# Stick-breaking attention in a two-block kernel: query tiles in rising order, scores one tile at a time, more projection chunks between them

## Chip, cores and metric

The kernel runs on one core of a Trainium2 chip. The metric is the device time of one execution in microseconds (us), as the median of several runs. The engines are TensorE (PE; PEld is its weight load), VectorE (DVE), ScalarE (ACT), GpSimd (POOL) and SyncE (SP), which issues the DMAs. Each engine works through its own queue in order.

## What is computed

Two transformer blocks on a sequence of T = 1024 with D = 1024, in fp32. The first block projects the normed input to the columns of three branches, two of them gated linear attention and the third stick-breaking attention with four heads of width 64, and projects the joined outputs. The second block (sparse and latent attention, feed-forward) is not touched by the change. The part that the change is about:

```python
def stick_breaking_attn(q, k, v):
    scale = dh ** -0.5
    for i in range(t // SB_BLOCK):                     # SB_BLOCK = 128
        n_keys = (i + 1) * SB_BLOCK
        z = jnp.einsum('bhtd,bhsd->bhts', q_blk, k[:, :, :n_keys]) * scale
        strict = s_pos < t_pos
        log_beta = jax.nn.log_sigmoid(z)
        log_1m_beta = jnp.where(strict, jax.nn.log_sigmoid(-z), 0.0)
        between = lax.cumsum(log_1m_beta, axis=3, reverse=True) - log_1m_beta
        weights = jnp.where(strict, jnp.exp(log_beta + between), 0.0)
        outs.append(jnp.einsum('bhts,bhsv->bhtv', weights, v[:, :, :n_keys]))
...
def first_block(...):
    h = rms_norm(x) * (1.0 + scale) + shift
    p = h @ w_in
    (qa, ka, va, lra, ga, qb, fb, ib, gb, qc, kc, vc, gc) = split_columns(p)
    o_a = rms_norm(chunk_gated_linear_attn(qa, ka, va, log_alpha)) * gla_norm_w * silu(ga)
    o_b = rms_norm(chunk_gated_linear_attn(silu(qb), k_b, ib, log_f)) * hgrn_norm_w * silu(gb)
    o_c = stick_breaking_attn(qc, kc, vc) * silu(gc)
    x = x + gate * (jnp.concatenate([o_a, o_b, o_c]) @ w_out)
```

## The kernel before, in words

**Chunks.** Matmuls run in a split form: each operand is a rounded part and a remainder, and three products are added. After the first columns, the rest of the first block's input projection is cut into 50 chunks in a queue, `fq`. A chunk of `unit_f` has 24 matmuls 128x512 (L515 to L517, PSUM tile `F_ps`), one of `unit_v` 48 matmuls 128x256 (L242 to L244, `v_ps`). `fill()` issues the next chunk at the place where it is called, and loads the weights (raw tile from DMA, ACT's cast L209, POOL's subtraction L210). Two PSUM buffers serve all chunks. ACT copies a finished chunk to a staging tile (L500, `F_st`, `v_st`) and SP stores it; the four chunks of the values `vc` are instead split into two parts by ACT (L958) and DVE (L959). Four chunks are issued ahead of the heads loop, 18 in it, and 28 in the steps of the linear attention behind it, one in each of 28 steps.

**Stick-breaking attention** (L817 to L941). The 32 query tiles of four heads are handled as 16 items (head, pair `ip` of tiles); tile t = 2 ip + w has 128 (t + 1) keys. `prep` (L826) loads and splits a head's queries and keys (ACT L835 and L837, DVE L836, POOL L838). For one tile `stage_a` makes the scores in PSUM (`sb_pb`, two buffers; L850, L851, mask L852) and ACT's Abs, Exp and Ln (L854 to L856); `stage_b` is DVE's L863, the scan L864 and the subtraction L865, after which the PSUM is free, and ACT's Exp L866. For each of 40 pairs (item, two key blocks) `stage_c` transposes the weights (L217 into `sb_pg`, one buffer), copies them (L882, on ACT or DVE) and splits them on POOL (L883, L884); `stage_d` makes the products L898 into `sb_po`, one buffer for two items; `finish` adds the halves (ACT L911, DVE L914).

**Order around it.** The pairs are taken in the order 0, 3, 2, 1. The scores of four tiles are made before the loop, and in it the two tiles of item i + 2 around the slots of item i; the loop has 40 slots, and `slot * 18 // 40` says behind which of them a chunk is issued. A scheduler places the instructions of each engine from the order of the calls, by modelled readiness.

**The linear attention** behind it runs through 28 levels (4 head pairs of 7), each with four stages that are one step apart: DVE L619, L621 and ACT L622 (a), products with the decay on POOL and DVE (L641, b), PE's L654 (c) and DVE's masked copy L663 into the score tile (d). Each step issues a chunk while there are any. When `fq` is empty, the finished outputs are split for the out-projection (`mix_split`, L760 and L762). The reductions L336 on DVE make the gate's vector while the first chunks run.

## Time and profile before

| | us |
|---|---|
| median of 3 runs (2431.04 to 2431.95) | 2431.05 |
| the profiled execution, its own time | 2437.99 |
| its span in the profile | 2436.2 |
| PE busy in it | 2259.0 (93%) |
| DVE busy | 1433.1 (59%) |
| ACT busy | 895.3 (37%) |
| POOL busy | 1166.3 (48%) |

The profile is one execution of the kernel on the chip; busy times are the union of an engine's instructions, and matmuls are pipelined, so a matmul's own duration is longer than the distance to the next. A row of the waits says what an engine waited for, on which instruction, for how long in all, how often and the longest. In the timelines, a row is start, duration, engine, line, operation and tiles, with the idle time ahead of it in brackets and what ended it. The granted clock is PE's, as a share of full speed: 1.0 is 2.4 GHz, 0.5 is 1.2 GHz.

### The profile page before, as it was taken

The page shows a single profiled execution, that of the slowest core. Times are in us where ns is not written, and L with a number is a line of the kernel's source. Part 1 is how long each engine was busy: PE and PEld are TensorE (multiplying, and loading weights), DVE is VectorE, ACT ScalarE, POOL GpSimd, SP SyncE. Part 2 cuts the span into 40 slices and gives each one's busy share as a digit, 9 for nine tenths or more (in the row PEclk, how much of TensorE's full clock was granted, in tenths as well). Part 3 has the DMA queues.
Part 4 walks back from the last instruction along what each step waited for, and adds up shares of the span by engine and source line. Part 5 has one row for each costly group of instructions (what it writes and reads, how often), then busy time and mean ns, then how long its engine had stood idle before and what let it go on. Part 6 is the DMA issues. An engine that isn't in the chain of part 4 may idle for free.

```text
span 2436.2 us, 30605 instructions
## 1 busy us (share of the span) xinstructions
PE 2259.0 (93%) x11689; PEld 1882.3 (77%) x11689; DVE 1433.1 (59%) x1990; ACT 895.3 (37%) x1467; POOL 1166.3 (48%) x924
## 2 busy tenths in 40 slices
PE   4969989999989999978999998999999999999998
PEld 3748878787768888767778887788888888888886
DVE  8566684848656447899967776535333333333335
ACT  4446632432313244765367777103211111111111
POOL 4236684545446354444357888530334443443341
PEclk9979999979889999989999999999999999999999
DMA  6432231213442112434351442340111111111112
GB/s 256 119 111 74 100 117 70 105 57 133 160 166 87 63 67 96 158 123 116 113 138 44 110 114 92 120 148 31 65 44 52 44 44 52 52 52 44 52 44 80
DMA packets 127200, 226.20 MB, mean 93 GB/s; under 512 B 48818, under 2 KB 73026, under 8 KB 126658
## 3 DMA queue, kind: packets, MB, share of 16 engines
q1 hardware_dynamic: 127042, 224.14, 27.4%
q8 instruction: 94, 1.54, 0.3%
q14 instruction: 64, 0.52, 0.1%
HBM read 169.47 MB, written 54.63 MB: 92 GB/s over the span
## 4 chain that ended last, share of the span: by engine, by line
PE 47%; DVE 8%; ACT 3%; issue 2%; POOL 1%; DMA 1%; SPq 0%; DVEq 0%; ACTq 0%; POOLq 0%
PE up_pb L1980 5%; PE up_pb L1979 5%; PE up_pb L1981 5%; PE br_ps L1925 3%; PE dn_ps L2034 3%; PE dn_ps L2036 3%; PE dn_ps L2035 3%; DVE topk_r L1589 2%; ACT topk_r L1590 1%; PE dn_pb L1980 1%; PE dn_pb L1981 1%; PE dn_pb L1979 1%; PE op_ps L1126 1%; PE op_ps L1125 1%; PE op_ps L1124 1%
## 5 line engine op out<-in xcount | busy, mean ns | idle before, releaser
L2038 DVE TENSOR_TENSOR br_h<-br_h,dn_ps 128x512 f32<-128x512 f32 x176 | 119.7, 686 | 237.4 <-PE dn_ps L2036 237.2
L205 POOL TENSOR_SCALAR up_wh<-up_raw 128x1024 fp32r<-128x1024 f32 x41 | 43.5, 1062 | 273.0 <-PE up_pb L1980 134.0
L2017 DVE SCALAR_TENSOR_TENSOR ffn_ws<-up_pb,cols,ffn_ws 128x1023 f32<-128x1023 f32 x66 | 84.6, 1282 | 138.9 <-ACT ffn_ws L2015 138.0
L2015 ACT ACTIVATE ffn_ws<-up_pb,cols 128x1024 f32<-128x1024 f32 x33 | 40.0, 1211 | 234.9 <-PE up_pb L1981 234.9
L1590 ACT ACTIVATE topk_r<-topk_r 128x896 bf16<-128x896 bf16 (+2 forms) x96 | 90.4, 945 | 61.6 <-DVE topk_r L1589 61.6
L210 POOL TENSOR_TENSOR up_wl<-up_raw,up_wh 128x1024 fp32r<-128x1024 f32 x41 | 98.4, 2401 | 20.2 <-PE up_pb L1981 17.5
L1980 PE MATMUL up_pb<-op_fl,up_wh 128*128 128x512 f32 x264 | 102.8, 389 | 0.0
L1981 PE MATMUL up_pb<-br_h,up_wl 128*128 128x512 f32 x264 | 102.8, 389 | 0.0
L1980 PE MATMUL up_pb<-br_h,up_wh 128*128 128x512 f32 x264 | 102.8, 389 | 0.0
L1981 PE MATMUL up_pb<-op_fh,up_wl 128*128 128x512 f32 x264 | 102.8, 389 | 0.0
L1979 PE MATMUL up_pb<-br_h,up_wh 128*128 128x512 f32 x264 | 102.8, 389 | 0.0
L1979 PE MATMUL up_pb<-op_fh,up_wh 128*128 128x512 f32 x264 | 102.8, 389 | 0.0
L2022 ACT CAST up_g<-ffn_ws 128x1024 fp32r<-128x1024 f32 x22 | 23.1, 1051 | 176.4 <-PE dn_ps L2035 98.0
L2034 PE MATMUL dn_ps<-dn_wh,up_g 128*128 128x512 f32 x192 | 75.2, 392 | 1.2 <-DVE br_h L2038 1.2
L2036 PE MATMUL dn_ps<-dn_wh,up_g 128*128 128x512 f32 x192 | 74.8, 390 | 0.0
L2035 PE MATMUL dn_ps<-dn_wl,up_g 128*128 128x512 f32 x192 | 74.8, 390 | 0.0
L2020 POOL TENSOR_TENSOR ffn_ws<-ffn_ws 128x1024 f32<-128x1024 f32 x22 | 52.7, 2396 | 32.7 <-DVE ffn_ws L2017 32.7
L883 POOL TENSOR_SCALAR sb_tmp<-sb_st 128x512 fp32r<-128x512 f32 (+1 forms) x40 | 36.9, 923 | 60.2 <-ACT sb_st L882 32.0
L1709 POOL TENSOR_TENSOR attB_pt<-attB_r,attB_pt 128x512 fp32r<-128x512 f32 (+1 forms) x54 | 63.5, 1175 | 4.1
L1436 DVE SCALAR_TENSOR_TENSOR c_isc<-idx_r,x_iws,c_isc 128x384 f32<-128x384 f32 (+5 forms) x42 | 46.7, 1111 | 30.5 <-ACT idx_r L1433 28.8
L1709 POOL TENSOR_TENSOR attA_pt<-attA_r,attA_pt 128x512 fp32r<-128x512 f32 (+1 forms) x52 | 61.5, 1183 | 4.0
L1670 DVE TENSOR_SCALAR_CACHE_REDUCE attB_g<-attB_pb 128x1024 f32<-128x1024 f32 (+3 forms) x64 | 47.7, 753 | 26.6 <-PE attB_pb L1663 23.7
(770 smaller groups left out, 7755.9 us busy)
## 6 DMA issues: line engine op xcount, KB each, us to landing
up_raw<-in_wu SPq DMA_DIRECT2D x43, 512.0 KB, 3.2
dn_raw<-in_wu SPq DMA_DIRECT2D x21, 512.0 KB, 3.3
sb_sp<-F_st SPq DMA_DIRECT2D x34, 256.0 KB, 2.0
init_X<-in_wada SPq DMA_DIRECT2D x13, 512.0 KB, 4.6
c_raw<-in_wu SPq DMA_DIRECT2D x13, 512.0 KB, 3.4
sb_raw<-in_wu SPq DMA_DIRECT2D x12, 512.0 KB, 4.3
br_raw<-in_wu SPq DMA_DIRECT2D x12, 512.0 KB, 4.3
bq_raw<-in_wu SPq DMA_DIRECT2D x11, 512.0 KB, 3.5
```

Of the source, the lines that this page charges most:

```text
L210: (nc.gpsimd if pool else nc.vector).tensor_tensor(l, raw, h, op=OP.subtract)
L1590: nc.scalar.activation(y, y, AF.Copy, accum_out=cnt[:, j:j + 1])
L1709: nc.gpsimd.tensor_tensor(lo, x, hi, op=OP.subtract)
L1925: nc.tensor.matmul(po, w[:, ws], x[:, k, hs], start=(n == 0), stop=(n == 11))
L1979: nc.tensor.matmul(o, wh[:, s], self.hh[h][:, kk], start=(kk == 0), stop=False)
L1980: nc.tensor.matmul(o, wh[:, s], self.hl[h][:, kk], start=False, stop=False)
L1981: nc.tensor.matmul(o, wl[:, s], self.hh[h][:, kk], start=False, stop=(kk == KT - 1))
L2017: nc.vector.scalar_tensor_tensor(u[:, d:], p[:, :T - d], tap(2 - d), u[:, d:], op0=OP.mult, op1=OP.add)
L2034: nc.tensor.matmul(po, hi[:, ts], wh[:, cs], start=(k == 0), stop=False)
L2035: nc.tensor.matmul(po, hi[:, ts], wl[:, cs], start=False, stop=False)
L2036: nc.tensor.matmul(po, lo[:, ts], wh[:, cs], start=False, stop=(k == 1))
L2038: nc.vector.tensor_tensor(x, x, po, op=OP.add)
```

## The change

The pairs are taken in rising order 0, 1, 2, 3. The scores of five single tiles are made ahead of the loop, with a chunk behind each of the second to the fifth; then the loop asks ahead of each slot for as many tiles as `5 + slot * 4 // 5` allows, so that four tiles fall on five slots, one at a time. The next head's `prep` is issued ahead of the scores of the second pair's first tile. In the 40 slots there are again 18 chunks, at `slot * 9 // 20`. In all, 26 chunks are issued by the end of the loop in place of 22, and 24 are left for the linear attention, whose last four of 28 steps have none. Because the pairs rise, `finish` writes 512 neighbouring columns. The split of a `vc` chunk is done in two pieces for each engine, of 128x4x64, in place of four of 128x2x64. Lines behind L822 have numbers lower by one.

```diff
-        order = (0, 3, 2, 1)
-        items = [(hd, ip) for hd in range(4) for ip in order]
+        items = [(hd, ip) for hd in range(4) for ip in range(4)]
...
-            po, n, place, end = live["po"], 0, int(ip > 1), 2 * ip + 1
+            po, n, place, end = live["po"], 0, ip % 2, 2 * ip + 1
...
-            if (h, ip) == (0, order[1]):
+            if (h, ip) == (0, 1):
                 live["o"] = self.gt("mx")
...
-            q2 = lambda y: y[hs].rearrange("p (q t) -> p q t", q=2)
-            o = live["o"][hs].rearrange("p (q t) -> p q t", q=4)[:, slice(1, 3) if ip in (1, 2) else slice(0, 4, 3)]
-            nc.vector.tensor_tensor(o, q2(po), q2(t1), op=OP.add)
-            if (h, ip) == (1, order[-1]):
+            nc.vector.tensor_tensor(live["o"][hs, ip // 2 * 512:ip // 2 * 512 + 512], po[hs], t1[hs], op=OP.add)
+            if (h, ip) == (1, 3):
                 done(pair, live["o"])
 
         yield prep(0)
 
-        for i in range(2):
-            for w in (1, 0):
+        ahead = [(i, w) for i in range(len(items)) for w in range(2)]
+
+        def scores(n):
+            while ahead and 2 * len(items) - len(ahead) < n:
+                i, w = ahead.pop(0)
+                if (items[i][1], w) == (1, 0) and items[i][0] < 3:
+                    prep(items[i][0] + 1)
                 stage_a(i, w)
                 stage_b(i, w)
-        behind, slot, slots = [], 0, 4 * 10
+        for n in range(1, 6):
+            scores(n)
+            if n > 1:
+                self.fill()
+        behind, slot = [], 0
         for i, (hd, ip) in enumerate(items):
-            if ip == order[0] and hd < 3:
-                prep(hd + 1)
             for c in range(ip + 1):
-                for w in (((1, 0) if ip == 0 else (1,)) if c == 0 else (0,) if c == (ip + 1) // 2 else ()):
-                    if i + 2 < len(items):
-                        stage_a(i + 2, w)
-                        stage_b(i + 2, w)
+                slot += 1
+                scores(5 + slot * 4 // 5)
                 stage_c(i, c)
                 behind.append((i, c))
-                slot += 1
-                if slot * 18 // slots > (slot - 1) * 18 // slots:
+                if slot * 9 // 20 > (slot - 1) * 9 // 20:
                     self.fill()
...
-                for c in range(2):
-                    nc.scalar.copy(hi[:, c], x[:, c])
-                    nc.vector.tensor_tensor(lo[:, c], x[:, c], hi[:, c], op=OP.subtract)
+                nc.scalar.copy(hi, x)
+                nc.vector.tensor_tensor(lo, x, hi, op=OP.subtract)
```

**Where instructions move.** Each list is the order of one engine's instructions, not a time. The first place is ACT at the start of the heads. Names: `v_ps` and `F_ps` are the chunks' PSUM tiles, `F_st` their staging tiles, `sb_pb` the scores of a tile (128 columns for each key block), `sb_X` and `sb_S` its weights, `sb_wh` a weight block of a chunk, `loga` the decay of the linear attention. Before:

```order
L958 CAST sb_w872_490<-v_ps139_831 128x2x64
L209 CAST sb_wh206_1208<-sb_raw205_1206 128x1024
L492 ACTIVATE loga_tmp135_816<-loga_tmp135_816 128x1024
L958 CAST sb_w872_490<-v_ps139_831 128x2x64
L958 CAST sb_w873_491<-v_ps139_831 128x2x64 x2
L854 ACTIVATE sb_X153_923<-sb_pb152_919 128x256
L855 ACTIVATE sb_X153_923<-sb_X153_923 128x256
L856 ACTIVATE sb_X153_923<-sb_X153_923 128x256
L209 CAST sb_wh209_1214<-sb_raw208_1212 128x1024
```

and some twenty rows later, still before, the first copy of an `F_ps` chunk, `F_ps182`:

```order
L854 ACTIVATE sb_S167_1003<-sb_pb166_997 128x640
L855 ACTIVATE sb_S167_1003<-sb_S167_1003 128x640
L856 ACTIVATE sb_S167_1003<-sb_S167_1003 128x640
L882 COPY sb_st178_1048<-sb_pg176_1042 128x512
L500 COPY F_st183_1083<-F_ps182_1058 128x512
L866 ACTIVATE sb_S165_989<-sb_S165_989 128x768
L866 ACTIVATE sb_S167_1003<-sb_S167_1003 128x640
```

After, the start of the heads:

```order
L958 CAST sb_w872_490<-v_ps139_819 128x4x64
L209 CAST sb_wh172_1027<-sb_raw171_1025 128x1024
L492 ACTIVATE loga_tmp135_804<-loga_tmp135_804 128x1024
L958 CAST sb_w873_491<-v_ps139_819 128x4x64
L500 COPY F_st160_958<-F_ps159_933 128x512
L209 CAST sb_wh175_1033<-sb_raw174_1031 128x1024
L500 COPY F_st168_1010<-F_ps167_985 128x512
L853 ACTIVATE sb_X153_907<-sb_pb152_903 128x128
L854 ACTIVATE sb_X153_907<-sb_X153_907 128x128
L855 ACTIVATE sb_X153_907<-sb_X153_907 128x128
L853 ACTIVATE sb_X155_919<-sb_pb154_915 128x256
L854 ACTIVATE sb_X155_919<-sb_X155_919 128x256
```

The copies of the first two chunks (`F_ps159`, `F_ps167`) now stand ahead of the first Abs of a score tile, and the split of the last `vc` chunk is two rows in place of four; before, the first such copy stood behind the functions of six tiles.

The second place is PE at the first tiles of the second head. Before, with the tiles of 256 and 128 keys (`sb_pb195`, `sb_pb200`), a transpose into `sb_pg` between them and the chunk `F_ps224` behind:

```order
L850 MATMUL sb_pb195_1158<-sb_qkb160_971,sb_qkb161_972 128x256
L851 MATMUL sb_pb195_1158<-sb_qkb160_971,sb_qkb162_973 128x256
L852 LDWEIGHTS idb_118
L852 MATMUL sb_pb195_1158<-neg_475,idb_118 128x128
L217 MATMUL sb_pg202_1196<-idr_116,sb_S167_1003 128x128
L217 MATMUL sb_pg202_1196<-idr_116,sb_S165_989 128x128
L850 MATMUL sb_pb200_1184<-sb_qkb160_971,sb_qkb161_972 128x128
L851 MATMUL sb_pb200_1184<-sb_qkb160_971,sb_qkb162_973 128x128
L852 LDWEIGHTS idb_118
L852 MATMUL sb_pb200_1184<-neg_475,idb_118 128x128
L516 MATMUL F_ps224_1292<-init_hl4_93,sb_wh180_1054 128x512
L517 MATMUL F_ps224_1292<-init_hh2_91,sb_wl181_1055 128x512
```

After, with the tiles of 256 and 384 keys (`sb_pb220`, `sb_pb231`) and matmuls of the chunk `v_ps241`:

```order
L849 MATMUL sb_pb220_1350<-sb_qkb161_961,sb_qkb162_962 128x256
L850 MATMUL sb_pb220_1350<-sb_qkb161_961,sb_qkb163_963 128x256
L851 LDWEIGHTS idb_118
L851 MATMUL sb_pb220_1350<-neg_475,idb_118 128x128
L217 MATMUL sb_pg222_1362<-idr_116,sb_X192_1146 128x128
L244 MATMUL v_ps241_1488<-sb_wh175_1033,init_hl4_93 128x256
L849 MATMUL sb_pb231_1440<-sb_qkb161_961,sb_qkb162_962 128x384
L850 MATMUL sb_pb231_1440<-sb_qkb161_961,sb_qkb163_963 128x384
L851 LDWEIGHTS idb_118
L851 MATMUL sb_pb231_1440<-neg_475,idb_118 128x128
L897 MATMUL sb_po219_1345<-sb_tmp217_1340,sb_w872_490 128x256
L242 MATMUL v_ps241_1488<-sb_wh175_1033,init_hh2_91 128x256
```

Before, no matmul of a chunk stood between the two tiles; after, one does here, while 22 to 38 stand between the tiles of the first head from the fifth on. Later in the phase both kinds occur.

The third place is ACT at the end of the linear attention, where L622 and L624 belong to a level of the linear attention, L701, L262 and L708 to a norm, L760 to the split for the out-projection and L738 to a gate. Before:

```order
L500 ACTIVATE F_st719_4659<-F_ps718_4634 128x512
L622 ACTIVATE gla64_X725_4685<-gla64_X725_4685 128x1024
L738 ACT_TABLE_LOAD
L738 ACTIVATE F_tmp720_4662<-mix_X721_4663 128x1024
L624 ACTIVATE gla64_X729_4730<-gla64_X729_4730 128x512
L760 CAST F_mh732_4761<-mix_tmp736_4765 128x512
L500 ACTIVATE F_st727_4714<-F_ps726_4689 128x512
L760 CAST F_mh732_4761<-mix_tmp737_4771 128x512
L760 CAST F_mh733_4762<-mix_tmp736_4765 128x512
L760 CAST F_mh733_4762<-mix_tmp737_4771 128x512
L500 ACTIVATE F_st731_4758<-F_ps730_4733 128x512
L760 CAST F_mh732_4761<-mix_tmp739_4790 128x512
```

After, the rows around the last copy of a chunk in the first block's projection:

```order
L622 ACTIVATE gla64_X722_4692<-gla64_X722_4692 128x1024
L760 CAST F_mh707_4613<-mix_tmp710_4616 128x512
L760 CAST F_mh707_4613<-mix_tmp711_4622 128x512
L500 ACTIVATE F_st705_4609<-F_ps704_4584 128x512
L701 ACTIVATE go64_tmp717_4648<-go64_mx701_4565 128x1024
L261 ACT_TABLE_LOAD
L760 CAST F_mh706_4612<-mix_tmp719_4667 128x512
L760 CAST F_mh707_4613<-mix_tmp719_4667 128x512
L262 ACTIVATE go64_c715_4646<-go64_pg714_4645,epsc_122 128x16
L708 ACTIVATE go64_c715_4646<-go64_c715_4646 128x16
L760 CAST F_mh706_4612<-mix_tmp720_4673 128x512
L760 CAST F_mh707_4613<-mix_tmp720_4673 128x512
L622 ACTIVATE gla64_X730_4751<-gla64_X730_4751 128x1024
```

Before, copies of chunks (L500) alternate with the splits L760 up to the last level's functions; after, the last one (`F_st705`) stands ahead of a further level's function L622 and most of the splits.

## Rows read from the trace of the kernel before

**Rows 1.** Windows: stretch, its length, busy us (count) of five engines, PEclk, DMA share, GB/s

```profile
117.00:142.00 25.00, 15.40 (x61) 11.85 (x59) 20.80 (x28) 7.01 (x15) 8.00 (x3) 0.84 0.64 225
142.00:170.00 28.00, 14.81 (x50) 10.94 (x50) 20.92 (x18) 17.20 (x22) 11.62 (x9) 0.53 0.14 44
170.00:230.00 60.00, 54.33 (x384) 49.40 (x383) 36.21 (x39) 38.00 (x65) 36.40 (x30) 0.94 0.20 62
230.00:290.00 60.00, 55.66 (x346) 48.81 (x345) 39.03 (x41) 38.71 (x65) 39.84 (x30) 0.94 0.35 123
290.00:351.00 61.00, 50.85 (x320) 44.10 (x318) 48.43 (x40) 29.22 (x42) 52.75 (x36) 0.99 0.25 91
351.00:613.00 262.00, 249.25 (x1437) 208.66 (x1438) 170.90 (x159) 85.01 (x100) 125.56 (x65) 0.91 0.26 92
613.00:651.00 38.00, 37.99 (x248) 32.94 (x247) 30.81 (x30) 16.09 (x21) 13.69 (x10) 1.00 0.38 139
651.00:684.00 33.00, 25.31 (x109) 15.56 (x110) 8.67 (x12) 10.38 (x16) 12.16 (x9) 0.53 0.65 236
684.00:2436.00 1752.00, 1678.77 (x8304) 1399.80 (x8302) 979.21 (x1517) 601.68 (x1043) 823.88 (x712) 0.99 0.25 82
```

**Rows 2.** PE's waits, 117 to 170 us: us in total, times, longest

```profile
PE sb_pb L850 <- DVE sb_X L865: 8.5, 3, 5.8
PE F_ps L515 <- DVE sb_w L959: 6.1, 1, 6.1
PE ada_po L217 <- DVE ada_c L336: 3.5, 1, 3.5
```

**Rows 3.** PE's timeline around the first chunks of the heads

```profile
117.51 0.48 PE L515 MATMUL F_ps<-init_hh,sb_wh 128*128 128x512 f32 x1
...
122.86 0.39 PE L517 MATMUL F_ps<-init_hh,sb_wl 128*128 128x512 f32 x1
129.38 0.77 PE L515 MATMUL F_ps<-init_hh,sb_wh 128*128 128x512 f32 x1 [6.13 <-DVE sb_w L959]
```

**Rows 4.** DVE's timeline, 117 to 142 us

```profile
117.36 3.04 DVE L336 CUSTOM_DVE_ANT_0 ada_X<-ada_X,init_mx 128x1024 f32<-128x1024 f32 x1
...
128.94 0.29 DVE L959 TENSOR_TENSOR sb_w<-v_ps,sb_w 128x128 fp32r<-128x128 f32 x1 [0.33 <-ACT sb_w L958]
...
134.67 0.69 DVE L864 TENSOR_TENSOR_SCAN sb_X<-sb_X 128x256 f32<-128x256 f32 x1
```

**Rows 5.** DVE's timeline at 231 us

```profile
230.68 2.23 DVE L864 TENSOR_TENSOR_SCAN sb_S<-sb_S 128x256 f32<-128x256 f32 x1
```

**Rows 6.** ACT's timeline, 117 to 170 us

```profile
131.73 0.38 ACT L854 ACTIVATE sb_X<-sb_pb 128x256 f32<-128x256 f32 x1 [2.82 <-DMA loga_sp<-loga_X]
...
164.40 0.59 ACT L500 COPY F_st<-F_ps 128x512 f32<-128x512 f32 x1
```

**Rows 7.** PE's waits, 170 to 351 us

```profile
PE sb_pb L850 <- DVE sb_S L865: 5.5, 2, 4.5
...
PE sb_pg L217 <- ACT sb_st L882: 2.5, 1, 2.5
```

**Rows 8.** DVE's groups by line, 613 to 651 us: busy, mean ns, idle before

```profile
L663 DVE COPY_PREDICATED ST<-lv,gla_pb 128x1024 f32<-128x1024 uint8 x6 | 8.9, 1481 | 3.0 <-PE gla_pb L654 3.0
L619 DVE TENSOR_TENSOR gla_X<-go_qkb 128x512 f32<-128x512 f32 x4 | 5.1, 1282 | 0.0
...
L621 DVE TENSOR_TENSOR gla_X<-go_qkb 128x512 f32<-128x512 f32 x3 | 2.1, 689 | 0.0
```

**Rows 9.** ACT's timeline, 608 to 655 us

```profile
623.43 0.60 ACT L500 ACTIVATE F_st<-F_ps 128x512 f32<-128x512 f32 x1
...
648.27 0.59 ACT L500 ACTIVATE F_st<-F_ps 128x512 f32<-128x512 f32 x1
```

**Rows 10.** POOL's groups by line and shape, 117 to 351 us

```profile
L884 POOL TENSOR_TENSOR sb_tmp<-sb_st,sb_tmp 128x512 fp32r<-128x512 f32 x24 | 34.1, 1419 | 1.7
...
L883 POOL TENSOR_SCALAR sb_tmp<-sb_st 128x512 fp32r<-128x512 f32 x24 | 21.2, 885 | 35.0 <-DVE sb_st L882 28.2 <-ACT sb_st L882 6.8
```

## The prediction

> **What bounds the kernel now.** I first read the busy time by stretch [rows 1]. From 684 us to the end TensorE (PE) works 1678.77 of 1752 us at a granted clock of 0.99, and from there on the instructions of every engine stand as they did; only what lies ahead can move. The heads of the attention fill 117 to 351 us. There PE's busy time is 15.40 + 14.81 + 54.33 + 55.66 + 50.85 = 191.05 us of 234, so 43 us are idle, and the first 53 us are the worst: 30.21 us of work, at clocks of 0.84 and 0.53, between 22.8 us of idle time. From 351 to 613 us PE is full (249.25 of 262). In 613 to 651 us PE is full too (37.99 of 38), while VectorE (DVE) is busy for 30.81. The last stretch, 651 to 684 us, is a chain of single steps at half clock.
>
> Next I ask what PE waited for in the first 53 us [rows 2]: 8.5 us until DVE's subtraction L865 gave a score tile's PSUM back, 6.1 us until L959 gave a chunk's PSUM back, 3.5 us for the gate's vector. The 6.1 us are seen one by one [rows 3, 4]: PE ends its chunk at about 123.2, the next starts at 129.38, and the last L959 stands at 128.94, behind a reduction L336 that takes 3.04 us. So the PSUM pair of the chunks is held by a piece that DVE does late, and on ScalarE (ACT) the first Abs of a score tile starts at 131.73 [rows 6]. The chunk that ended at 123.2 is copied out by ACT only at 164.40 [rows 6], behind the functions of six score tiles: all that time one of the two PSUM buffers is simply parked.
>
> **The price of a chunk.** Its first matmul starts at 117.51 and its 24th at 122.86 and takes 0.39 us [rows 3]: 5.7 us with the end, and 5.35 x 24/23 = 5.6 us from start to start. I use 5.6 us for both kinds of chunk.
>
> **The change part by part.** *Four more chunks among the first score tiles.* They take 4 x 5.6 = 22.4 us of PE into this phase and out of the steps of the linear attention. In ACT's new order the copies out of the first two chunks stand ahead of the first Abs, and the merged copies L958 don't alternate with DVE any more, so a buffer comes free before PE asks for the third. By 170 us PE had done some 2.46 chunks, 13.8 us, and about 8 us of scores, transposes and products: 21.8 us of work at full speed in 53. I walked the new orders with the durations of the rows: four chunks back to back from 117.5 to 140 (the first Abs of before starts at 131.73 only, and DVE is busy for 20.80 of the 25 us up to 142, mostly with reductions like L336's, so the scores lose little), then score tiles with a third of a chunk or more between them. That gives about 4.3 more chunks by 170, 24 us, with the attention as far as before; 21.8 + 24 = 46 of 53 us. PE then has no long gap, and the half clock of 142 to 170 (0.53) goes with it. Bounds: if only the 6.1 us of L959, the 3.5 us and half of the 8.5 us fill, 14 us; if all the idle time fills and the clock is full, 53 - 21.8 = 31 us. I take 24, since the order leaves no row behind which a parked buffer stands. The second weight block for these chunks has to be loaded and split earlier; the DMA engines are busy for 0.64 of 117 to 142 [rows 1], so there is room, and were it late the chunks would fall into two and two with a gap like the 6.1 us of before, which is inside these bounds. Of these 24 us the four chunks use 22.4; the sum is **-1.6 us** (+8 to -9).
>
> *The merged pieces L958 and L959.* Four pieces of each become two for the last projection tile; this belongs to the 6.1 us above and is counted there.
>
> *One score tile at a time, in rising order.* From 170 to 351 us the idle time is 5.67 + 4.34 + 10.15 = 20.2 us [rows 1]. The two waits that a pair of tiles makes are named: PE's third tile waits until DVE has worked off the first, 5.5 us, and a transpose waits 2.5 us for ACT's copy, which stands behind a pair's functions [rows 7]. Spacing removes the reason for both: **-8 us**. Bounds: nothing, since in the new order some tiles still stand in pairs with a single projection matmul between them; and -15 with the other waits on the copies and on POOL. No matmul, copy or scan is dropped, so there is no gain in work. The contiguous last addition per pair of items has the same 512 columns as before: 0.
>
> *The preparation of the next head* moves from the head's start to the second tile of its second item. Its four loads, ACT's two casts, the subtraction L836 and POOL's L838 are the same ones, in the same queues, and are wanted only six tiles later: 0, covered by the three or so chunks that lie between. Were the cover gone, the first tile of each of three heads would wait; the nearest row is L850's longest wait, 5.8 us [rows 2].
>
> *The tail of the linear attention.* The queue of chunks is now empty after the 24th of 28 steps. Before, ACT still copied chunks out from 623.43 to 648.27 [rows 9], the first and the last of the four of this stretch, so 4 x 5.6 = 22.4 of PE's 38 us there were chunks. Without them PE has 16 us of work, and the next bound is DVE with 30.81 us [rows 1], most of it L663 at 1.48, L619 at 1.28 and L621 at 0.69 us [rows 8]. So of 22.4 us taken out only 38 - 31 = 7 can come back, and as the six copies of L663 wait for products of PE in turn I take **-6 us**. Bounds: 0, if the chain of steps is as long without chunks; -12, if L619 fell to the 0.69 us of L621 and DVE's other rows lost their company with POOL likewise (some 26 us).
>
> Sum: -1.6 - 8 - 6 = -15.6, rounded to **-15 us**. The profiled execution took 2437.99 us, so it would be 2423; the median of the runs is 7 us lower, 2431.05, and gives **2416 us**.
>
> **What the Trainium skill says against it.** The same scan takes 0.69 us for 256 columns at 134.67 and 2.23 us at 230.68 [rows 4, 5], 1.5 us more, the second beside a subtraction of POOL. The Trainium skill, page "SBUF — State Buffer", section "Who interferes with whom", says that a DVE instruction with two inputs in SBUF contends with a GpSimd instruction that reads SBUF, and that the one issued later waits. By that rule the second scan met POOL, and a denser phase would have more such meetings; the third rival is this mechanism. In 651 to 684 us PE shows a clock of 0.53 although it is busy for 25.31 of 33 us [rows 1], with idle gaps between short steps. The Trainium skill, page "TensorE: Matmul & The Clock Gate", section "What's actually happening", says that the throttled clock is the default and activity releases it. By that rule the chunks keep the tail's clock at 1.00, and taking them away costs what they freed; the second rival is this one.
>
> **The rivals.**
> 1. *All waits go.* The first 53 us fill wholly (-9), the 15 us after 170 go, and the tail falls to -12 with DVE undisturbed; not all at once, so some -30: **2401**. For it: none of these waits is on data that is truly late. Against it: one buffer for transposes and one for products stay.
> 2. *The tail gives nothing back.* PE's 16 us without chunks are 32 at half clock, beside DVE's 31, and each step waits for the other: 38 stay 38. Only the phase of the heads gains, 1.6 + 8: **2422**. For it: 651 to 684 us [rows 1] is just such a stretch. Against it: four stages of the steps are in flight at once.
> 3. *DVE becomes the bound of the heads.* DVE is busy there for 20.80 + 20.92 + 36.21 + 39.03 + 48.43 = 165 us of 234. With tiles spread evenly, scans meet POOL's L884 (1.42 us) and L883 (0.88 us [rows 10]) more often. My forecast leaves the phase at 224 us, so this decides from 59 us more on DVE, 1.5 us for each of the 40 transposed pieces. If each piece cost DVE the 2.2 to 2.3 us that POOL works on it (88 us in all), DVE had 253 us: +19 in place of -9.6, with the tail's -6 some +13: **2444**.
> 4. *The spacing isn't there.* The engines' orders come from a scheduler, and if its pairs stay, only the chunks move: -1.6, and with the tail's 6 lost as in the second rival it is **2430**, no change.
>
> **How the numbers follow.** What tells from no change here is about 0.2%, 4.9 us: faster is below 2426.2, slower above 2435.9. Forecast 0.52, first rival 0.14, second 0.13: faster 0.79. Fourth 0.12: the same. Third 0.09: slower. The range takes the forecast's bounds, the second rival, most of the fourth and the nearer part of the first: 2402 to 2430, which leaves out the third rival and parts of the first and fourth, some 0.2.
>
> **What would show it.** In the changed kernel's profile PE should be busy for over 40 of the 53 us from 117 on, with a clock above 0.9 in 142 to 170, four chunks without a gap over 1 us, and no copy L500 over 10 us late. The wait of L850 (now L849) on DVE after 170 us should fall from 5.5 to under 2 us. The phase of the heads should end at about 341 us (351 less 9.6), with 26 chunks done in place of 22. The last chunk should be copied out some four steps ahead of the end of the linear attention, and the stretch behind it should be one in which DVE is over 0.9 busy. The out-projection, which begins at 684 us before [rows 1], should begin near 669. I am wrong if scans grow so that DVE passes 200 us in the phase (third rival), if PE in the tail is at half clock and DVE idle (second), or if the waits on L865 stay (fourth).

## The result

The changed kernel took 2401.39 us, the median of 4 runs (2395.36 to 2410.10), against 2431.50 (2431.04 to 2436.55) before; the ratio is 0.9874, 95% interval 0.9839 to 0.9910. So it is 30 us faster, twice the 15 us forecast, and 0.6 us below the low end of the range. In a second set of runs it was 2407.15 against 2435.39, ratio 0.9883 (0.9853 to 0.9913). The profiled execution took 2410.10 us, 27.9 less than the profiled execution before, with a span of 2408.2. Both profiled executions are longer than their kernel's median (by 6.5 and 8.7 us), so what follows divides the 27.9 us between two single executions; how the 30 us of the medians divide is known only as far as further profiles repeat it.

The windows of the changed kernel, in the stretches and columns of [rows 1] (stretch, its length, busy us and count of PE, PEld, DVE, ACT and POOL, granted clock of PE, DMA share, GB/s):

```profile
117.00:142.00 25.00, 22.59 (x99) 18.41 (x98) 20.94 (x28) 9.35 (x18) 8.17 (x3) 0.93 0.79 291
142.00:170.00 28.00, 27.53 (x206) 25.23 (x205) 19.22 (x18) 20.66 (x30) 12.12 (x10) 1.00 0.23 68
170.00:230.00 60.00, 55.04 (x341) 47.53 (x340) 42.09 (x47) 37.91 (x67) 44.00 (x32) 0.97 0.28 88
...
351.00:613.00 262.00, 250.49 (x1402) 205.19 (x1400) 176.12 (x177) 97.50 (x117) 129.91 (x70) 0.91 0.26 91
613.00:651.00 38.00, 26.73 (x121) 17.32 (x122) 22.59 (x13) 3.19 (x5) 17.45 (x11) 0.54 0.12 41
```

In the first 53 us PE is now busy for 22.59 + 27.53 = 50.1 us, against 30.2, and the clock of 142 to 170 is 1.00 in place of 0.53. In 613 to 651 it is the other way round: 26.73 us of work at 0.54, where before PE was full at 1.00 [rows 1].

PE's waits of the changed kernel from 117 to 170 us, the answer to [rows 2]: instruction, what it waited for, us in all, times, longest:

```profile
PE F_ps L515 <- DVE sb_w L959: 2.4, 1, 2.4
PE sb_po L897 <- POOL sb_tmp L883: 0.5, 1, 0.5
```

and from 170 to 351 us, the answer to [rows 7]:

```profile
PE sb_pg L217 <- ACT sb_st L881: 5.2, 4, 3.0
PE F_ps L515 <- ACT v_st L500: 3.9, 2, 3.2
...
PE sb_pb L849 <- DVE sb_X L864: 1.5, 4, 0.6
PE sb_pb L849 <- DVE sb_S L864: 1.0, 1, 1.0
```

The waits for a score tile's PSUM (8.5 us ahead of 170, 5.5 behind it) are 0 and 2.5 us. The 3.9 us for a chunk's copy (L500) are new; 3.2 of them lie behind the last product of the heads.

Fixed stretches of the clock cut through different work in the two kernels, so from here on the span is cut at events: the first score matmul; the last product of the heads (345.0 us before, 338.0 after); the linear attention's first masked copy L663 (361.3, 344.4); the last masked copy of its third pair of heads (589.2, 575.2) and of its fourth (651.8, 632.0); the first matmul of the out-projection (683.6, 663.0); the end. "Joint" is what lies between the heads and the first masked copy.

| us, profiled executions | before | after | moved | forecast |
|---|---|---|---|---|
| heads | 228.0 | 220.6 | -7.4 | -9.6 |
| joint | 16.3 | 6.4 | -9.9 | 0 |
| levels of the first three pairs | 227.9 | 230.8 | +2.9 | 0 |
| levels of the fourth pair | 62.6 | 56.8 | -5.8 | -6, with the next |
| their end, to the out-projection | 31.8 | 31.0 | -0.8 | |
| out-projection and all behind it | 1752.6 | 1745.2 | -7.4 | 0 |

The three terms of the sum are there with nearly their sizes, -14.0 in place of -15.6. The other half of the gain lies in two rows for which the forecast had no term. The joint and the three pairs behind it have to be read together, since PE works at chunks in both: counted by their matmuls, the kernel before did 1.46 chunks in the joint and 18.79 in the three pairs, the changed one 0.35 and 19.88. For the same 20.2 chunks the two rows together are 7.0 us shorter.

### The profile page after: what moved, and what is told of

Read it like the earlier page. It is cut to its first block, busy times and chain, and to the rows that moved or that the text cites. A ratio compares the mean times of both kernels' runs of the same rounds, so it can differ in the third digit from the quotient of the medians.

```text
span 2408.2 us, 30577 instructions
## 1 busy us (share of the span) xinstructions
PE 2255.4 (94%) x11689; PEld 1880.8 (78%) x11689; DVE 1413.2 (59%) x1982; ACT 892.4 (37%) x1459; POOL 1169.6 (49%) x924
## 4 chain that ended last, share of the span: by engine, by line
PE 51%; DVE 5%; ACT 2%; issue 2%; POOL 1%; DMA 0%; POOLq 0%; DVEq 0%; ACTq 0%; SPq 0%
PE up_pb L1981 5%; PE up_pb L1979 5%; PE up_pb L1980 5%; PE br_ps L1925 3%; PE dn_ps L2034 3%; PE dn_ps L2036 3%; PE dn_ps L2035 3%; PE F_ps L230 2%; PE F_ps L228 2%; PE F_ps L229 2%; DVE topk_r L1589 2%; PE dn_pb L1980 1%; PE dn_pb L1981 1%; PE dn_pb L1979 1%; PE op_ps L1126 1%
## 5 line engine op out<-in xcount | busy, mean ns | idle before, releaser
L2015 ACT ACTIVATE ffn_ws<-up_pb,cols 128x1024 f32<-128x1024 f32 x33 | 40.0, 1212 | 235.0 <-PE up_pb L1981 235.0
L210 POOL TENSOR_TENSOR up_wl<-up_raw,up_wh 128x1024 fp32r<-128x1024 f32 x41 | 98.5, 2403 | 20.2 <-PE up_pb L1981 17.5
L242 PE MATMUL v_ps<-sb_wh,init_hh 128*128 128x256 f32 x256 | 75.1, 294 | 0.7 <-ACT v_st L500 0.7
L244 PE MATMUL v_ps<-sb_wh,init_hl 128*128 128x256 f32 x256 | 75.3, 294 | 0.0
L243 PE MATMUL v_ps<-sb_wl,init_hh 128*128 128x256 f32 x256 | 74.4, 291 | 0.7 <-POOL sb_wl L210 0.7
L210 POOL TENSOR_TENSOR sb_wl<-sb_raw,sb_wh 128x1024 fp32r<-128x1024 f32 x15 | 39.7, 2651 | 60.3 <-ACT sb_wh L209 41.7
L654 PE MATMUL gla_pb<-QB,gla_X 128*128 128x128 f32 x448 | 62.2, 291 | 6.5 <-POOL gla_X L643 6.5
```

What stands on the lines that cost most here:

```text
L210: (nc.gpsimd if pool else nc.vector).tensor_tensor(l, raw, h, op=OP.subtract)
L242: nc.tensor.matmul(po, hh[:, k, ts], wh[:, cs], start=(k == 0), stop=False)
L244: nc.tensor.matmul(po, hl[:, k, ts], wh[:, cs], start=False, stop=(k == KT - 1))
```

## The parts alone

All kernels of this and the next sections are compared with the kernel before, run beside them; the stretches are of one profiled execution each and stand in a table behind the runs.

**Chunks alone.** To the kernel before, in its old order of tiles:

```diff
             for w in (1, 0):
                 stage_a(i, w)
                 stage_b(i, w)
+                self.fill()
```

> The kernel before with one chunk more behind each of its first four score tiles (26 chunks in the heads, 24 in the linear attention); order and pairs as before. If the chunks are half the gain (my steps): the four chunks cost the phase of the heads 22.4 us and find about that much idle time, so the heads end within 3 us of 351, the tail behind them is 6 to 13 us shorter, 2418 to 2424 us in all. If the chunks are the whole gain, 2401 to 2406 us. If they only displace work (the one parked PSUM buffer is still behind the score functions on ACT), the heads end 10 us or more later and the time is 2428 us or more.

Measured: 2416.53 us against 2435.39, ratio 0.9925 (0.9897 to 0.9952), 18 us faster, just below the first answer's range. The heads were 0.6 us shorter than in the first profile of before with 3.7 chunks more done in them, so the forecast's -1.6 fits; the heads of the old order scatter by 4 us, though (228.0 to 232.3 in the table below). The last levels gave 5.9 us. The rest is the joint (7.2 us) and the stretch behind the out-projection (1748.4).

**Order alone.** The changed kernel without the chunks among its first tiles:

```diff
         for n in range(1, 6):
             scores(n)
-            if n > 1:
-                self.fill()
```

> The changed kernel without the four chunks among its first tiles (22 chunks in the heads as before, 28 in the linear attention). If spacing and order are half the gain (my steps): the heads end 8 us or more ahead of 351, the first 53 us stay idle in part, the tail is as before, 2415 to 2424 us. If the order alone does nothing without chunks between the tiles: 2428 to 2434 us. If the whole gain is the order's: 2401 to 2406 us.

Measured: 2419.77 us, ratio 0.9943 (0.9919 to 0.9966), 14 us faster. But the heads (226.1 us) gained 1.9 us only against the first profile of before, and 4 us against the mean of the five profiles whose heads are as before (230.3): PE was busy for 36.73 of the first 53 us and waited 6.5 us for the gate's vector. With chunks between the tiles the order is worth more: from chunks alone (227.4 us) to both (220.6 and 219.3) it is 7 to 8 us. The joint is 4.3 us and the last levels are as before (62.6). The two gains sum to 32 us, where both together give 28; that is not more than the intervals allow. The table does show the joint and the last stretch shorter with either part alone, so these cannot be won twice.

**The merge alone.** The kernel before with the split of the value chunks in two pieces per engine:

```diff
-                for c in range(2):
-                    nc.scalar.copy(hi[:, c], x[:, c])
-                    nc.vector.tensor_tensor(lo[:, c], x[:, c], hi[:, c], op=OP.subtract)
+                nc.scalar.copy(hi, x)
+                nc.vector.tensor_tensor(lo, x, hi, op=OP.subtract)
```

> The kernel before with only the merged split of the value chunks (two pieces of 128x4x64 for each engine in place of four of 128x2x64). My steps count it inside the 6.1 us that PE waited at 129.38: if a buffer then comes free, that wait goes and the heads end up to 6 us earlier; the parked buffer and the ada reductions stay, so I expect 2427 to 2432 us. If the merge is a main part of the gain: below 2420 us.

Measured: 2427.15 us (12 runs, 2416.03 to 2434.17), ratio 0.9960 (0.9940 to 0.9980). The time lies at the low end of the first answer, but the kernel before was 2435.39 us in these runs, so the gain is 8 us, more than the 6.1 us of the wait. The wait on L959 fell from 6.1 to 2.4 us, as in the changed kernel, and yet the heads of the profiled execution (one of the longer of these runs, 2431.98) were 235.2 us, 3 to 7 us longer than in the profiles of the old order; against that, its joint was 9.1 us and its last stretch 1747.1. One profile doesn't say where the 8 us of the median come from.

**The changed kernel without the merge**, the same edit undone:

> The changed kernel without the merged split of the value chunks (four pieces again). If the merge only frees one buffer early, at the start of the heads: the first 53 us lose up to 6 us, 2401 to 2413 us. If it is a part of the gain of its own, as the 8 us of the kernel before with the merge alone: 2408 us or more.

Measured: 2407.19 us, ratio to the kernel before 0.9901 (0.9874 to 0.9928): with the other two parts in place the merge is worth nothing that these runs can tell. The heads were 224.1 us, 4 us more than with it.

**The changed kernel again.**

> The changed kernel once more, for its spread and for the stretch from the out-projection's first matmul to the end, whose instructions are ordered as before: it took 1752.6 us in the profile of before and 1745.2 in that of after. If this difference belongs to the change, the stretch is 1744 to 1747 us again; if it is chance of how DVE and POOL meet, it lies anywhere from 1744 to 1755 us, and the kernel's time moves with it between 2395 and 2412 us.

Measured: 2407.15 us (2396.52 to 2413.56); the last stretch was 1748.4 us, outside the first answer and inside the second. The same instructions in the same order now took 219.4 us for the levels of the first three pairs, where the first profile had 230.8. The windows of the two executions for these levels, columns as above, first the changed kernel's first profile, then this one:

```profile
344.40:575.20 230.80, 223.61 (x1203) 184.84 (x1202) 151.45 (x150) 81.74 (x93) 118.93 (x61) 0.90 0.26 92
```

```profile
343.60:563.00 219.40, 210.66 (x1201) 175.24 (x1200) 151.94 (x151) 81.50 (x93) 118.44 (x61) 0.96 0.28 96
```

DVE does the same 151 us in both; the granted clock is 0.90 and 0.96. So 11 us of difference in this stretch come and go with PE's clock in one and the same kernel, and no cause is to be sought for a difference of that size there.

The stretches of all runs, in us:

| kernel | heads | joint | three pairs | fourth pair | end | behind | top-k in it |
|---|---|---|---|---|---|---|---|
| before | 228.0 | 16.3 | 227.9 | 62.6 | 31.8 | 1752.6 | 235.5 |
| before, again | 232.3 | 16.4 | 220.8 | 63.7 | 31.5 | 1753.0 | 233.1 |
| after | 220.6 | 6.4 | 230.8 | 56.8 | 31.0 | 1745.2 | 228.6 |
| after, again | 219.3 | 6.4 | 219.4 | 56.7 | 31.0 | 1748.4 | 229.0 |
| chunks alone | 227.4 | 7.2 | 228.9 | 56.7 | 31.0 | 1748.4 | 228.6 |
| order alone | 226.1 | 4.3 | 229.5 | 62.6 | 33.6 | 1746.2 | 228.8 |
| merge alone | 235.2 | 9.1 | 225.4 | 62.6 | 33.3 | 1747.1 | 228.7 |
| after without merge | 224.1 | 6.4 | 215.7 | 56.5 | 31.0 | 1749.0 | 228.7 |
| before, ACT order at joint | 231.4 | 16.3 | 230.7 | 62.6 | 31.7 | 1755.3 | 235.0 |
| before, POOL relieved at joint | 229.7 | 13.3 | 222.2 | 62.7 | 31.8 | 1752.7 | 237.0 |
| before, both at joint | 230.2 | 14.5 | 216.4 | 62.7 | 31.4 | 1749.7 | 228.5 |
| after, chunks in all steps | 219.3 | 6.4 | 211.1 | 67.5 | 33.1 | 1750.4 | 228.7 |
| after, 29 chunks in heads | 231.1 | 5.7 | 211.3 | 58.4 | 30.8 | 1753.3 | 228.7 |

The last levels repeat to 0.3 us: 62.6 with their four last chunks, 56.7 without (63.7 once). That term of the forecast is shown. The second profiles of the two kernels differ by -13.0 us in the heads, -10.0 in the joint, -1.4 in the three pairs, -7.5 in the fourth pair and its end, and -4.6 behind. So the heads' and the tail's terms, the joint and a part of the last stretch repeat; their sizes repeat to within 6 us.

## The joint

Between the heads and the first level stands DVE's masked copy L606, which writes the diagonal into a tile of 128x2048. Its row in the kernel before, and POOL's rows beside it (start, duration, engine, line, operation):

```profile
351.98 9.28 DVE L606 COPY_PREDICATED ST<-idm,gs_c 128x2048 f32<-128x2048 uint8 x1
```

```profile
351.86 2.36 POOL L574 TENSOR_TENSOR gs_tmp<-gs_tmp,sb_qkb 128x1024 f32<-128x1024 f32 x1
354.18 2.36 POOL L210 TENSOR_TENSOR gla_wl<-gla_raw,gla_wh 128x1024 fp32r<-128x1024 f32 x1
356.50 2.40 POOL L563 TENSOR_TENSOR gs_tmp<-gla_qkb,gla_qkb 128x1024 f32<-128x1024 f32 x1
```

and of the kernel after:

```profile
339.86 3.74 DVE L606 COPY_PREDICATED ST<-idm,gs_c 128x2048 f32<-128x2048 uint8 x1
```

```profile
339.78 1.50 POOL L643 TENSOR_TENSOR gla_X<-gla_X,sb_qkb 128x512 f32<-128x512 f32 x1 [1.72 <-ACT gla_X L622]
341.23 4.58 POOL L210 TENSOR_TENSOR gla_wl<-gla_raw,gla_wh 128x1024 fp32r<-128x1024 f32 x1
```

Before, L606 began 0.1 us behind the first of three POOL instructions that follow one another, and ended 2.4 us behind the last; after, it stood behind one of 1.50 us, and POOL's next one took 4.58 in place of 2.36 us. L606 also began 7.0 us behind the last product before, and 1.9 us after. 5.1 + 5.5 us is the joint's 9.9, within a microsecond. The 5.1 us are DVE's rows between its last subtraction L621, which ends 0.5 to 0.7 us behind the last product in both kernels, and L606. Before:

```profile
345.45 1.65 DVE L641 TENSOR_TENSOR QB<-gla_X,sb_qkb 64x512 f32<-64x512 f32 x1
347.13 2.18 DVE L572 TENSOR_TENSOR gs_tmp<-sb_qkb 128x1024 f32<-128x1024 f32 x1
351.04 0.69 DVE L914 TENSOR_TENSOR sb_mx<-sb_po,sb_st 64x512 f32<-64x512 f32 x1 [1.73 <-ACT sb_st L911]
```

and after:

```profile
338.53 1.21 DVE L572 TENSOR_TENSOR gs_tmp<-sb_qkb 128x1024 f32<-128x1024 f32 x1
343.63 0.69 DVE L911 TENSOR_TENSOR sb_mx<-sb_po,sb_st 64x512 f32<-64x512 f32 x1
```

The half product L641 (1.65), 1.0 us more for L572, the wait for ACT's L911 (1.73) and the halves' addition L914 (0.69) stand ahead of L606 before and not after. Are these rows of DVE and POOL what makes the joint long, or is it PE's wait of 3.6 us for a chunk's copy in the same place? PE's wait in the joint of the kernel before:

```profile
PE v_ps L242 <- ACT F_st L500: 3.6, 1, 3.6
```

**Before once more.**

> The kernel before once more, for a second profile of it. From the last product of the heads to the linear attention's first level it took 16.3 us, and from the out-projection to the end 1752.6 us, against 6.4 and 1745.2 after. If both belong to the order of before, they are 15 to 17 and 1751 to 1754 us again; if the second is chance of how VectorE and GpSimd meet, it is 1745 to 1749 us here as in the four other variants.

Measured: 2437.93 us, one run. Both stretches repeat, 16.4 and 1753.0 us, L606 with 9.30.

**ACT's order at the joint.** To the kernel before, a rule of order alone: ACT's L573 behind the last L911 and the next L500.

```diff
...
+        if getattr(self, "kd_exp", None) is not None:
+            self.after(self.kd_exp, i)
+            self.kd_exp = None
...
-        nc.scalar.activation(kd, kd, AF.Exp, scale=sc)
+        x = nc.scalar.activation(kd, kd, AF.Exp, scale=sc)
+        if self.last_fin is not None:
+            self.after(x, self.last_fin)
+            self.kd_exp, self.last_fin = x, None
...
```

> The kernel before with one edit in ACT's order at the end of the heads: the linear attention's Exp L573 stands behind the last halves' copy L911 and the next copy of a chunk L500, where it stood ahead of both. If that order makes the joint long (PE waited 3.6 us for that L500 and its clock then fell), the joint falls from 16 us to 7 to 10 us and the kernel gains 4 to 9 us. If the joint is long because DVE and POOL meet there (L606 took 9.28 us), it stays above 13 us and the gain is under 3 us.

Measured: 2433.04 us against 2430.40, ratio 1.0001 (0.9982 to 1.0020). PE's wait for L500 was gone and the joint stayed at 16.3 us. L606 (its line here is L612) began 5.3 us behind the last product in place of 7.0, and now had four whole POOL instructions beside it:

```profile
356.16 10.95 DVE L612 COPY_PREDICATED ST<-idm,gs_c 128x2048 f32<-128x2048 uint8 x1
```

So PE's wait was not what made the joint long, and an earlier start of L606 was taken back by a longer stand beside POOL.

**POOL relieved at the joint.** To the kernel before, two of the three products beside L606 on DVE:

```diff
-        nc.gpsimd.tensor_tensor(pr, q, k, op=OP.mult)
+        self.ngs = getattr(self, "ngs", 0) + 1
+        (nc.vector if self.ngs == 2 else nc.gpsimd).tensor_tensor(pr, q, k, op=OP.mult)
...
-        nc.gpsimd.tensor_tensor(kd, kd, k, op=OP.mult)
+        (nc.vector if self.ngs == 1 else nc.gpsimd).tensor_tensor(kd, kd, k, op=OP.mult)
```

> The kernel before with two multiplications at the joint (L574 of the first pair of heads, L563 of the second) on DVE in place of POOL, so that one POOL instruction is left beside DVE's masked copy L606 in place of three; PE's and ACT's order stay. If L606 is long because it stands still while POOL's subtractions and products run, it falls from 9.3 to 3.5 to 5 us, and the joint from 16.3 to 10 to 13 us with the 2 to 3 us of the moved product paid on DVE ahead of it. If the 9.3 us are its own at that place (the first writing of the tile), it stays at 9 us and the joint grows by 1 to 4 us.

Measured: 2431.07 us against 2432.99, ratio 0.9988 (0.9968 to 1.0008). L606 (L607 here) and POOL's subtraction, DVE's row first:

```profile
359.08 2.45 DVE L607 COPY_PREDICATED ST<-idm,gs_c 128x2048 f32<-128x2048 uint8 x1
```

```profile
359.19 4.55 POOL L210 TENSOR_TENSOR gla_wl<-gla_raw,gla_wh 128x1024 fp32r<-128x1024 f32 x1 [4.51 <-ACT gla_wh L209]
```

That is shown: all but 2.45 of the 9.28 us were POOL's, since L606 takes 2.45 us, as its three later ones do in the same execution (2.47 to 2.48), where it starts ahead of POOL, and then POOL's instruction takes 4.55. The Trainium skill, page "SBUF — State Buffer", section "Who interferes with whom", says of a DVE instruction in its two-port modes that whoever issues first gets the pair of ports shared with GpSimd for the whole instruction while the other blocks; the section does not name the masked copy, but these two rows look like it. The kernel before goes beyond it: there L606 had begun at 351.98, ahead of POOL's second and third instruction (354.18, 356.50), and ended behind both, while after the change POOL's second one (341.23) ended behind L606. Which of the two goes ahead in such a row these runs do not explain. L606 now began 10.8 us behind the last product, since the moved products and the longer subtractions stand ahead of it, so the joint fell by 3 us only, to 13.3, and the kernel gained nothing that can be told.

**Both edits.** The edits of the two last kernels together:

> The kernel before with both edits of the joint together: ACT copies the chunk out ahead of L573, and L574 of the first pair and L563 of the second run on DVE, so that L606 has less of POOL beside it. Alone the first took PE's wait away and left the joint at 16.3 us, the second took L606 from 9.28 to 2.45 us and left 13.3 us, with PE waiting 6.7 us. If the joint is the longer of these two chains, together they give 8 to 11 us and a kernel 5 to 8 us faster than before. If a third chain (DVE's list of the first levels ahead of L606) sets it, it stays at 12 to 13 us and the gain is under 3 us.

Measured: 2428.56 us against 2431.13, ratio 0.9990 (0.9973 to 1.0007). The joint was 14.5 us, longer than the third answer's 12 to 13 us, but its gain of under 3 us holds, and the first answer's 8 to 11 us are excluded. Ahead of L606, DVE works without a gap over 0.1 us from 340.79 to 357.2 us through the first levels' subtractions, the half product, and L572 (L576 here):

```profile
346.52 2.91 DVE L626 TENSOR_TENSOR gla_X<-sb_qkb 128x512 f32<-128x512 f32 x1
349.35 1.76 DVE L628 TENSOR_TENSOR gla_X<-sb_qkb 128x512 f32<-128x512 f32 x1
351.13 1.65 DVE L648 TENSOR_TENSOR QB<-gla_X,sb_qkb 64x512 f32<-64x512 f32 x1
352.81 3.66 DVE L576 TENSOR_TENSOR gs_tmp<-sb_qkb 128x1024 f32<-128x1024 f32 x1
```

Behind this list, L606 (L613 here) took 4.31 us beside a POOL instruction that began 0.4 us ahead of it:

```profile
359.06 4.31 DVE L613 COPY_PREDICATED ST<-idm,gs_c 128x2048 f32<-128x2048 uint8 x1
```

```profile
358.68 2.36 POOL L210 TENSOR_TENSOR gla_wl<-gla_raw,gla_wh 128x1024 fp32r<-128x1024 f32 x1 [3.29 <-ACT gla_wh L209]
```

So the joint before is DVE's list up to L606 and L606's stand beside POOL, and each edit only moves the place at which the two meet; the edits that relieve POOL put their products on this list. After the change, L606 stands ahead of the last halves' addition in DVE's queue (339.86 and 343.63 us), and before behind it. That the change came with this order is seen in the traces. No kernel here gives this order of DVE to the kernel before, so that the order alone is worth the joint's gain is read from the rows and not shown, and why the scheduler chose it was not tried. The pairs' rising order is not needed for it: with chunks alone the joint is 7.2 us, with the merge alone 9.1. What follows for the forecast: a joint of 16 us whose end DVE sets could be read in the kernel before, and an edit that changes the order there can move it.

## Behind the out-projection

From the out-projection on, both kernels have the same instructions, and the forecast took their order and time as given. The table's last column is the top-k search in that stretch, from its first L1589 to its last L1613. It takes 228.5 to 229.0 us in nine profiles and 233.1 to 237.0 in four. In it DVE is busy for 218.98 of 235.50 us in the kernel before. It meets POOL's splits of weight blocks; the last of four long meetings of L1579 in the kernel before, DVE's rows and POOL's:

```profile
1154.04 1.03 DVE L1594 TENSOR_SCALAR topk_tk<-topk_tk 128x6 int32<-128x6 f32 x1
1155.10 0.17 DVE L1595 COPY_PREDICATED topk_tk<-topk_tk,topk_tk 128x6 int32<-128x6 int32 x1
1155.31 2.26 DVE L1579 TENSOR_SCALAR topk_tk<-topk_tk 128x6 int32<-128x6 int32 x1
```

```profile
1153.99 1.05 POOL L205 TENSOR_SCALAR F_wh<-F_raw 128x1024 fp32r<-128x1024 f32 x1 [4.24 <-PE F_ps L229]
1155.13 2.41 POOL L210 TENSOR_TENSOR F_wl<-F_raw,F_wh 128x1024 fp32r<-128x1024 f32 x1
```

An instruction on six columns, which takes 0.17 us in most of its 31 places, takes 2.26 us beside POOL's subtraction of a weight block. Over the stretch 984 to 1220 us in the kernel before, and 960 to 1190 us in the changed one, the groups of this line and of L1609 (count, busy us, mean ns) are, first before, then after:

```profile
L1579 DVE TENSOR_SCALAR topk_tk<-topk_tk 128x6 int32<-128x6 int32 x31 | 14.5, 469 | 1.1
L1609 DVE TENSOR_SCALAR topk_jk<-c_isc,topk_tk 128x384 bf16<-128x384 f32 (+5 forms) x6 | 7.5, 1257 | 0.2
```

```profile
L1579 DVE TENSOR_SCALAR topk_tk<-topk_tk 128x6 int32<-128x6 int32 x31 | 10.3, 334 | 1.1
L1609 DVE TENSOR_SCALAR topk_jk<-c_isc,topk_tk 128x384 bf16<-128x384 f32 (+5 forms) x6 | 3.5, 584 | 0.2
```

Those two lines are 8.2 us of DVE, where the search is 6.9 us longer. L1579 is the steadier mark: it is 14.5 us in all four long searches, since four of its 31 instructions take 2.2 to 2.3 us, and 10.3 to 12.4 in the nine short ones, with two or three such; in the second profile of before L1609 took 3.5 us as after. So the search has two courses, a long one in which the weight splits hit more such instructions, and a short one.

The order is not quite the same, either. In the search of the changed kernel one copy on ACT (L1531) and one addition on POOL (L1269) stand a few places later. POOL before, some 408 us behind the start of the out-projection:

```profile
1091.31 0.84 POOL L1269 TENSOR_TENSOR c_s<-c_ru,c_rw 128x128 f32<-128x128 f32 x1
1092.11 0.91 POOL L1268 TENSOR_TENSOR c_rw<-c_s,rope_ss 128x64 f32<-128x64 f32 x2
```

and after:

```profile
1068.10 1.30 POOL L1268 TENSOR_TENSOR c_rw<-c_s,rope_ss 128x64 f32<-128x64 f32 x2
1069.36 0.87 POOL L1269 TENSOR_TENSOR c_s<-c_ru,c_rw 128x128 f32<-128x128 f32 x2
```

All eight profiles with this later place have the short course; of the five with the place of before, four have the long one. The fifth, the kernel before with both edits at the joint, has the short one, so the later place is not needed for it. Whether it is enough, no run tries alone. Nor is the rising order of the pairs needed, since the merge alone takes the short course too. The rest of this stretch, without the search, scatters by 9 us (1515.7 to 1524.6 us in the 13 profiles). Of the 7.4 us in the result's table, up to 6.9 are the search's; the two profiles each of before and after differ by 4 to 8 us. What decides the course stays open.

## Can more be had

**Chunks in all steps of the linear attention**, on the changed kernel:

```diff
-                self.fill(-(-left // max(nfill - n, 1)))
+                self.fill((n + 1) * 6 // 7 - n * 6 // 7 if n < nfill else left)
```

> The changed kernel with its last 24 chunks spread over all 28 steps of the linear attention (none in each seventh step), in place of one in each of the first 24. If a chunk costs its 5.6 us where PE is full and some 1.5 us in the last steps, where DVE is the bound (56.7 us without four chunks, 62.6 with them), the steps ahead gain up to 22 us and the last ones lose 6: 2386 to 2398 us. If the steps are bound by DVE and by the chain of a level throughout: 2400 to 2412 us, as the changed kernel.

Measured: 2405.38 us, ratio to the kernel before 0.9887 (0.9868 to 0.9907), no better than the change (0.9874 and 0.9883). The three pairs fell to 211.1 us, and the fourth rose to 67.5 and its end to 33.1. By the count of its matmuls the fourth pair holds 4.58 chunks here and 1.88 in the changed kernel, so each of the 2.7 costs 13 / 2.7 = 4.8 us there, not 1.5. The number of chunks alone does not make this price: the kernel before has 5.96 chunks in its fourth pair and needs 62.6 and 31.8 us. What makes these steps long here is not shown.

**Three more chunks in the heads**, 21 in the 40 slots, and 21 in the linear attention:

```diff
-                if slot * 9 // 20 > (slot - 1) * 9 // 20:
+                if slot * 21 // 40 > (slot - 1) * 21 // 40:
...
-                self.fill(-(-left // max(nfill - n, 1)))
+                self.fill((n + 1) * 7 // 8 - n * 7 // 8 if n < nfill else left)
```

> The changed kernel with three more chunks in the heads' 40 slots (21) and the remaining 21 in the first 24 steps of the linear attention, none in each eighth. The spread over the steps showed the steps ahead 4 us shorter for each chunk left out, so three give 10 to 14 us. If the 15 us in which PE is still idle in the heads take the three in half, the heads lose 5 to 10 us: 2395 to 2403 us. If DVE's own work is what sets the heads, the three cost nothing there: 2388 to 2395 us. If each costs its 5.6 us: 2403 to 2410 us.

Measured: 2408.91 us, ratio 0.9907 (0.9891 to 0.9924). The heads grew from 220 to 231.1 us, 4 us for each of the three; PE was busy for 216.22 of them at a clock of 1.00, and the time lies in the third answer. PE is without work for 14.9 us in these heads, as long as in the changed kernel's: the three chunks did not get into that time, and that they cost less than 5.6 us each goes with a mean clock of 1.00 in place of 0.97. No kernel here beats the changed one.

## Why the prediction was right and wrong

- **What failed.** "Only what lies ahead can move" put nothing for the stretch from the out-projection on, and the sum had no term for the joint between the heads and the first level. Measured, the first moved by -7.4 us (-4.6 in the second profiles) and the joint by -9.9, or -7.0 with the levels that took over a chunk of its work. The orders behind 684 us are nearly the same, but their time is not: the search there takes 4 to 8 us more or less as DVE's small instructions meet POOL's. A nearly same order was taken for a same time. What decides between the two courses of the search, and whether DVE's order alone shortened the joint, stays open.
- **The four chunks.** Right. By 170 us PE had done 7.0 chunks in place of 2.46, 4.5 more where 4.3 were forecast; alone they changed the heads by -0.6 us (forecast -1.6), on a scatter of 4 us. The wait on L959 didn't go wholly: 2.4 of 6.1 us stay.
- **One tile at a time.** Right in size with chunks between the tiles (7 to 8 us against 8); alone it is 2 to 4 us, which the text didn't say. The size did not come by the two waits that were named: those of L850 on L865 fell from 5.5 to 2.5 us (forecast under 2), but those of transposes for ACT's copies grew from 2.5 to 5.2, so the two together are 7.7 us in place of 8.0. From 170 us to the last product PE's idle time fell from 17.2 to 12.0 us, by waits that the forecast did not name: for DVE's copies L882 (3.5 to 1.6 us), for POOL (2.5 to 0.5) and for the halves' addition L914 (2.4 to nothing). That the number fits is in part luck.
- **The joint.** No term at all, and -9.9 us. The prediction ended the heads at 351 us and took the steps behind them as unchanged. In the kernel before PE's 3.6 us and L606 with four times its later durations stood in that place. Taking PE's 3.6 us away gained nothing; L606's place in DVE's list is what the rows show in the shorter joints.
- **The tail.** Right: -6.6 us against -6, and 56.5 to 56.8 us for the fourth pair in four profiles without its last four chunks. DVE became the bound, as the forecast has it: from just behind the last chunk to the last masked copy it is busy for 30.52 of 31.30 us (columns as above).

```profile
600.70:632.00 31.30, 18.18 (x136) 17.11 (x134) 30.52 (x25) 12.01 (x18) 24.30 (x16) 0.71 0.40 143
```

  The clock did fall, as the second rival has it (0.71 in this stretch), and PE's waits on DVE and POOL rose, but the steps were shorter all the same.
- **The rivals.** The first gave 2401, the time that was measured, but not by its mechanism: PE still has 14.9 us without work in the heads, and the tail gave 6.6 of 12 us. The third did not come: the 32 scans took 52.6 us in all, against 55.1 before. Its mechanism, DVE standing beside POOL, did move time, but the other way and outside the heads: at L606 in the joint and at L1579 in the search the two met less. The fourth fell with the heads' waits.
- **The range** held the bounds of each term and nothing for the terms set to nought, and nothing for the kernel's own spread, which is 15 us in the four runs of after.

## What to carry to other kernels

Before an edit's terms are summed, look for rows in which an instruction takes several times its shortest duration in the same kernel (here 9.28 against 2.45 us, and 2.26 against 0.17): here each was a meeting of two engines that came and went with edits elsewhere, so it belongs into the range with both signs, in stretches that the edit does not touch too. Compare the orders of the untouched stretch instruction by instruction before its time is taken as given. Work moved into a stretch is free only as far as it gets into the engine's idle time: four chunks cost the heads nothing, three more cost 4 us each and left 14.9 us idle. Parts of a change that are measured alone need not add up, when each of them shortens the same stretch. And a stretch that got shorter has gained only what its neighbour did not take over: the joint's -9.9 us carried a chunk of work with it.

## What was not expected of the hardware

A DVE instruction on 128x6 elements took 0.17 us in most places and 2.26 us beside a POOL subtraction of 2.41 us. A DVE masked copy of 128x2048 took 2.45 us ahead of POOL's instruction, 3.74 and 4.31 behind one, 9.28 beside three in a row and 10.95 beside four; where DVE went ahead, POOL's subtraction took 4.55 or 4.58 in place of 2.36 us. One kernel's same stretch of 219 or 231 us ran at a mean granted clock of 0.96 or 0.90 in two executions.
